# Hybrid decoder step: TensorE keeps the source's order through the units of the RWKV layer

## The chip, the core and the metric

The kernel runs on one core of a Trainium2 chip. The metric is the device time of one execution in microseconds (us). Five engines run beside each other, each with its own queue of instructions that it takes in order: TensorE (PE; its weight loads are PEld), VectorE (DVE), ScalarE (ACT), GpSimd (POOL) and SyncE (SP, which issues most DMAs). Between engines, semaphores order the work.

## What is computed

One inference step of two layers for a prompt of 1024 tokens and a group of 8 single-token samples. Layer 0 is a convolution branch and a sparse-attention branch. Layer 1, which the change touches, is RWKV-7 time mixing:

```
x_prev = concat([shift_prev, x[:, :-1]]);  xsh = x + (x_prev - x) * mu      # six mixtures
r, k, v, z = xsh[:4] @ w_rkvz                                              # four dense projections
decay = exp(-exp(-softplus(-(w0 + tanh(xsh[4] @ w1) @ w2)) - 0.5))         # low-rank (lora)
a = sigmoid(a0 + (xsh[5] @ a1) @ a2)                                       # low-rank (lora)
kk = normalised(k * k_k);  k = k * (1 + (a - 1) * k_a)
for each token t:
    sa = S @ kk[t]
    S  = S * decay[t] - sa (kk[t] * a[t])^T + v[t] k[t]^T                  # state per head, 64 x 64
    y[t] = S @ r[t]
y = group_norm(y) + sum(r * k * r_k) * v
out = (y * silu(z)) @ w_out                                                # dense, then LayerNorm
```

All values are float32. A dense product is made of three products of halves: each operand is split into a high part and a low remainder (`xh`, `xl`, `wh`, `wl`), and `xh*wh + xl*wh + xh*wl` is added up.

## The kernel before, in words

`phase_d` computes layer 1. The 1024 tokens and 16 heads are cut into 16 **units**: 8 groups of 128 tokens times 2 halves of the heads. In a unit the recurrence is worked in chunks of 64 tokens with small matrices. The work of a unit stands in four generators, which yield between their steps:

- `s1`, the **preparation** (L1329 and on): loads k, a, sigma, r of the unit (`kt`, `at`, `st_`, `rt`), builds the normalised key and the running decays (`ss` and `cum`, two sums on TensorE into the PSUM tile `sm`; pool `pm` has one buffer of it), then `KBK` and `AM` on VectorE (L1369 to L1377), then gram products into `pa` (L1396), whose evictions give `AB`, `AM`, `MRB`, then transposes into `pa` (L1419, L1420). `AB` goes out to DRAM as `md` and comes back as `MT`.
- `s2`, the **solve**: a triangular inverse of small blocks, on VectorE alone (L1433 to L1436); the result goes to DRAM (`ud`) and comes back as `UT`.
- `joinUT`, the **join**: four groups of tiny products into `pg` (L1477, L1485, L1500, L1508), with copies and 32x32 transposes on VectorE between them.
- `s3`, the **state steps**: per chunk, products with the state into `pA` and `pB`, a copy `E` on VectorE (L1529), products with `UT`, copies into `SV` (L1538, L1539), products for the new state and the output (L1547, L1548); then a group norm with two sums (L1551, L1559).

Beside the units there is a queue `F1` of **dense** generators. `t_proj(h, nm, i)` is a projection of one half of the tokens: `xmake` mixes eight tiles of input (L1207 ACT, L1208 DVE, L1211 ACT, L1212 POOL) into the pool `dx` (nine buffers each of `xh` and `xl`), `wsplit` loads and splits a weight tile of 512 KB, and 24 products (`mm3`, L1184 to L1186) make one group, sixteen groups a projection. `t_sigma` and `t_a` are the lora branches: `lora_hidden` with its own `xmake`, then small products group by group (L1276, L1294). `t_out` is the output projection of 256 tokens (groups of 12 products of 512 columns, L1772 to L1774) with LayerNorm; `t_last` that of the last 256 (L1701 to L1703). `sample_d` does the samples' step.

The loop over units runs eight **slots** per unit. A slot calls one step of `s3` of unit u, of `joinUT` and `s2` of unit u+1, of `s1` of unit u+2, and lets `run` take dense steps from `F1` for a cost of `RATE` (1.2 in the first six units, then 1.1); a step costs what it yields, 1.0 if nothing.

What sets the order on the engines: the program is traced in the order of the source, and a scheduler then arranges each engine's queue by priority and by its own estimate of when operands are ready. It may move products of different generators past each other. `tc.keep_in_program_order` pins an instruction behind the one that was traced before it on the same engine.

Of the kernel before, what the change touches and what calls it, by code (L numbers as in the profile page):

```python
# [730 lines left out]
RATE = 1.2, 1.1  # L731
# [366 lines left out]
def phase_d(nc, tc, I, O, G):  # L1098
    C = G.C
    ident = C["ident"]  # L1100
    scr = G.scr
    HV = ((slice(0, 64), 0), (slice(64, 128), 1))
    flat = lambda t: t.rearrange("p a b -> p (a b)")
    with ExitStack() as es:
# [76 lines left out]
        def mm3(dst, wh, wl, x, lo, hi):  # L1181
            xh, xl = x
            for k in range(8):
                nc.tensor.matmul(dst, lhsT=wh[:, k], rhs=xh[k][:, lo:hi], start=k == 0, stop=False)  # L1184
                nc.tensor.matmul(dst, lhsT=wh[:, k], rhs=xl[k][:, lo:hi], start=False, stop=False)  # L1185
                nc.tensor.matmul(dst, lhsT=wl[:, k], rhs=xh[k][:, lo:hi], start=False, stop=k == 7)  # L1186
# [31 lines left out]
        def lora_hidden(h, src, i):  # L1218
# [10 lines left out]
            for _, g, lo, hi in chunks(h):  # L1229
                sl, r = slice(lo, hi), hi - lo  # L1230
                ph = acc()
                for k in range(8):
                    if k < 7:
                        nc.tensor.matmul(ph[:, 0:r], lhsT=W[:, k], rhs=xh[k][:, sl], start=k == 0, stop=False)
                    nc.tensor.matmul(ph[0:64, 0:r], lhsT=W[:, k, 0:64], rhs=xl[k][:, sl], start=False, stop=False)
                    if k == 7:
                        nc.tensor.matmul(ph[:, 0:r], lhsT=W[:, k], rhs=xh[k][:, sl], start=False, stop=True)
# [12 lines left out]
        def lora_w2(nm):  # L1250
# [15 lines left out]
        def t_sigma(h):  # L1266
# [4 lines left out]
            for ti, (o, r) in enumerate(toks):  # L1271
                for c in range(2):
# [3 lines left out]
                    nc.tensor.matmul(p[0:r], lhsT=H1[:, o:o + r], rhs=A[:, sl], start=True, stop=False)  # L1276
                    nc.tensor.matmul(p[0:r], lhsT=H2[:, o:o + r], rhs=B[:, sl], start=False, stop=True)
# [6 lines left out]
        def t_a(h):  # L1284
# [3 lines left out]
            for j in range(8):  # L1288
# [3 lines left out]
                for _, g, lo, hi in chunks(h):  # L1292
                    p = acc()
                    nc.tensor.matmul(p[:, 0:hi - lo], lhsT=A[:, sl], rhs=H1[:, lo:hi], start=True, stop=False)  # L1294
                    nc.tensor.matmul(p[:, 0:hi - lo], lhsT=B[:, sl], rhs=H2[:, lo:hi], start=False, stop=True)
# [32 lines left out]
        def s1(g, d, J):  # L1328
# [21 lines left out]
            nc.tensor.matmul(ss, lhsT=K["bones"], rhs=flat(inv), start=True, stop=True)  # L1350
# [4 lines left out]
            for m in range(4):  # L1355
                nc.tensor.matmul(cum[:, m * 128:m * 128 + 128], lhsT=st_[:, m], rhs=K["tri"], start=True, stop=True)
# [21 lines left out]
            yield  # L1378
            rk = t2("inv")
            nc.vector.tensor_tensor(rk, rt, kp, op=MUL)  # L1380
# [597 lines left out]
```

## Time and profile before

| | |
|---|---|
| median of 3 runs | 2209.96 us (2204.72 to 2212.83) |
| the profiled execution | 2201.91 us, span 2200.2 us |
| granted TensorE clock, mean | 0.871 |
| busy share of PE, DVE, ACT, POOL | 84%, 68%, 52%, 44% |

The spans of the table of stretches are counted from the first instruction. The loop over units takes the second half of the span. A matmul's busy time is modelled: it includes the time from its issue until its result is through, so products that follow each other overlap, and the distance between their starts says more than their duration. The clock is granted at two levels, 1.2 and 2.4 GHz; the column PEclk is the mean share of the upper one.

### The profile page before, as it was taken

To read this page: it belongs to the slowest core of one execution; us is meant where nothing else is said; L and a number is where in the kernel's file an instruction comes from. 1 tells how busy PE (TensorE), PEld (TensorE's weight loads), DVE (VectorE), ACT (ScalarE), POOL (GpSimd) and SP (SyncE) were. 2 spreads that over 40 slices of the span, in tenths; PEclk is the share of its full clock that TensorE was granted. 3 is DMA by queue.
4 is the path that set the end of the run, shared out by engine and by line. 5 is a ranking of instruction groups with operands and counts; after the bars stand their busy time and mean duration, and the time that the engine had idled before them with its cause. 6 is when DMAs were issued, how large, how long until landed. Compare 5 with 4: busy or idle time off the path is not lost. (4 is left out here: it accounts for less than half of the span.)

```text
span 2200.2 us, 41365 instructions
## 1 busy us (share of the span) xinstructions
PE 1844.0 (84%) x16026; PEld 1545.8 (70%) x16026; DVE 1491.9 (68%) x2543; ACT 1153.6 (52%) x2359; POOL 972.8 (44%) x784
## 2 busy tenths in 40 slices
PE   5988897668999997897887999897999787987865
PEld 5987896656767886674777987695888666875543
DVE  5998995557788878226364378827748987387453
ACT  3323324544665545357466467747754575465344
POOL 4667667554655545445345212323334434113233
PEclk9998998867999876898898999897899986988956
DMA  6424344521221213546556344433544544353333
GB/s 240 132 72 142 131 151 154 200 74 33 65 59 50 58 34 97 175 126 210 167 179 204 126 118 116 145 100 117 149 130 121 180 115 135 97 155 115 119 112 103
DMA packets 232095, 275.27 MB, mean 125 GB/s; under 512 B 71545, under 2 KB 171569, under 8 KB 227738
## 3 DMA queue, kind: packets, MB, share of 16 engines
q1 hardware_dynamic: 210712, 215.21, 32.1%
q0 software_dynamic: 7616, 41.52, 5.6%
q10 hardware_dynamic: 13570, 15.90, 2.0%
q8 instruction: 126, 2.06, 0.4%
q14 instruction: 71, 0.58, 0.1%
HBM read 212.47 MB, written 64.27 MB: 126 GB/s over the span
## 5 line engine op out<-in xcount | busy, mean ns | idle before, releaser
L121 POOL TENSOR_TENSOR wl<-w,wh 128x1024 fp32r<-128x1024 f32 x81 | 200.2, 2473 | 333.5 <-ACT wh L113 317.8
L1184 PE MATMUL mm<-xh,wh 128*128 128x256 f32 (+1 forms) x1024 | 308.3, 302 | 22.6 <-ACT og L1319 9.3
L1185 PE MATMUL mm<-xl,wh 128*128 128x256 f32 (+1 forms) x1024 | 300.9, 294 | 2.0 <-POOL xl L1212 1.1
L1186 PE MATMUL mm<-xh,wl 128*128 128x256 f32 (+1 forms) x1024 | 298.5, 293 | 3.5 <-POOL wl L121 3.5
L113 ACT ACTIVATE wh<-w 128x1024 fp32r<-128x1024 f32 (+2 forms) x130 | 134.4, 1036 | 208.2 <-PE mm L1185 60.9
L1184 PEld LDWEIGHTS mm<-xh,wh 128*128 128x128 f32 x1024 | 201.9, 198 | 35.8 <-ACT og L1319 12.0
L1185 PEld LDWEIGHTS mm<-xl,wh 128*128 128x128 f32 x1024 | 203.2, 198 | 5.4 <-issue 2.0
L1186 PEld LDWEIGHTS mm<-xh,wl 128*128 128x128 f32 x1024 | 202.1, 198 | 6.3 <-POOL wl L121 4.4
L268 DVE SCALAR_TENSOR_TENSOR c<-U,cw,c 128x1024 f32<-128x1024 f32 x120 | 198.0, 1674 | 0.9
L604 POOL TENSOR_TENSOR Pl<-PT,Ph 128x512 fp32r<-128x512 f32 (+1 forms) x102 | 131.9, 1298 | 150.4 <-DVE Ph L603 123.9
L252 POOL TENSOR_TENSOR cbuf<-cbuf 128x256 f32<-128x256 f32 (+2 forms) x72 | 131.3, 1829 | 85.2 <-ACT cbuf L250 82.3
L217 PE MATMUL S<-xh,wh 128*128 128x344 f32 (+1 forms) x432 | 146.6, 339 | 21.1 <-ACT wh L113 19.4
L219 PE MATMUL S<-xh,wl 128*128 128x344 f32 (+1 forms) x432 | 145.4, 337 | 15.7 <-POOL wl L121 11.6
L218 PE MATMUL S<-xl,wh 128*128 128x344 f32 (+1 forms) x432 | 146.3, 339 | 3.8 <-POOL xl L121 3.6
L1212 POOL TENSOR_TENSOR xl<-xs,xh 128x520 fp32r<-128x520 f32 (+1 forms) x76 | 104.6, 1382 | 91.2 <-ACT xh L1211 89.1
L250 ACT ACTIVATE cbuf<-cbuf,wrow 128x256 f32<-128x256 f32 x192 | 79.3, 496 | 112.1 <-DMA cbuf<-in_ccmp,cix 70.3
L1208 DVE SCALAR_TENSOR_TENSOR xs<-xk,mu,xs 128x512 f32<-128x512 f32 x96 | 92.7, 973 | 56.4 <-ACT xs L1207 55.7
L217 PEld LDWEIGHTS S<-xh,wh 128*128 128x128 f32 (+1 forms) x432 | 85.6, 198 | 23.2 <-ACT wh L113 21.9
L562 DVE TENSOR_REDUCE nm<-S 128x1 f32<-128x640 f32 (+7 forms) x128 | 88.3, 699 | 18.9 <-PE S L558 17.7
L219 PEld LDWEIGHTS S<-xh,wl 128*128 128x128 f32 (+1 forms) x432 | 84.9, 197 | 20.1 <-POOL wl L121 13.6
L121 DVE TENSOR_TENSOR wl<-w,wh 128x1024 fp32r<-128x1024 f32 x45 | 60.4, 1341 | 54.1 <-ACT wh L113 53.9
L218 PEld LDWEIGHTS S<-xl,wh 128*128 128x128 f32 (+1 forms) x432 | 84.8, 196 | 7.1 <-POOL xl L121 4.4
(610 smaller groups left out, 5399.3 us busy)
## 6 DMA issues: line engine op xcount, KB each, us to landing
w<-in_w_rkvz SPq DMA_DIRECT2D x64, 512.0 KB
w<-in_w_out SPq DMA_DIRECT2D x36, 512.0 KB
w<-in_w_fm SPq DMA_DIRECT2D x25, 512.0 KB
xk<-x1T SPq DMA_DIRECT2D x48, 260.0 KB
xk<-x1T SPq DMA_DIRECT2D x48, 256.0 KB
w<-in_w_out SPq DMA_DIRECT2D x16, 256.0 KB
x<-in_xp SPq DMA_DIRECT2D x8, 512.0 KB
x<-x ACTq DMA_DIRECT2D x8, 512.0 KB
```

The lines of the kernel that those rows point to most:

```text
L113: nc.scalar.activation(hi, src, AF.Copy, **({} if scale is None else {"scale": scale}))
L121: e_lo.tensor_tensor(lo, src, hi, op=SUB)
L217: nc.tensor.matmul(dst, lhsT=wh[:, k, 0:n], rhs=xh[:, k, sl], start=k == 0, stop=False)
L218: nc.tensor.matmul(dst, lhsT=wh[:, k, 0:n], rhs=xl[:, k, sl], start=False, stop=False)
L219: nc.tensor.matmul(dst, lhsT=wl[:, k, 0:n], rhs=xh[:, k, sl], start=False, stop=k == 7)
L252: nc.gpsimd.tensor_tensor(bv[:, 0:n], bv[:, 0:n], bv[:, n:2 * n], op=ADD)
L268: e.scalar_tensor_tensor(c[:, i, 0:T], u[:, k:k + T], cwh[:, i, k:k + 1], c[:, i, 0:T], op0=MUL, op1=ADD)
L604: lambda: nc.gpsimd.tensor_tensor(Pl[:, 0:w], PT[:, 0:w], Ph[:, 0:w], op=SUB)]
L1184: nc.tensor.matmul(dst, lhsT=wh[:, k], rhs=xh[k][:, lo:hi], start=k == 0, stop=False)
L1185: nc.tensor.matmul(dst, lhsT=wh[:, k], rhs=xl[k][:, lo:hi], start=False, stop=False)
L1186: nc.tensor.matmul(dst, lhsT=wl[:, k], rhs=xh[k][:, lo:hi], start=False, stop=k == 7)
L1212: (nc.vector if early[0] and k % LD == 0 else nc.gpsimd).tensor_tensor(lo[k][:, 0:n], t[:, 0:n], hi[k][:, 0:n], op=SUB)
```

## The change: what it does

Inside the loop over units every product and transpose of `phase_d` on TensorE is pinned to the order of the source (`tmm`, `ttr`, switched on by `order[0] = True` just ahead of the loop). The source is put in another order to go with it: `among` runs a lora branch inside the projection that follows it; the weights of the lora branches move from the buffers `wh`, `wl` to `big`; `joinUT` starts one slot earlier but gives its first slot to VectorE alone; `s1` has one yield moved and one dropped; `t_proj` charges 2.0 for the mixing of its input, `t_out` 0.25 per pair of tiles; `RATE` is 1.3 and 0.95; `t_out(2)` enters the queue at unit 14 instead of 13.

```diff
-RATE = 1.2, 1.1
+RATE = 1.3, 0.95
...
+    order = [False]
+
+    def ordered(f):
+        def g(*a, **k):
+            x = f(*a, **k)
+            return tc.keep_in_program_order(x) if order[0] else x
+        return g
+
+    tmm, ttr = ordered(nc.tensor.matmul), ordered(nc.tensor.transpose)
...
-                nc.tensor.matmul(dst, lhsT=wh[:, k], rhs=xh[k][:, lo:hi], start=k == 0, stop=False)
+                tmm(dst, lhsT=wh[:, k], rhs=xh[k][:, lo:hi], start=k == 0, stop=False)
...
-            A = flat(wp.tile([128, 8, 128], F32R, name="wh"))
+            A = flat(bp.tile([128, 8, 128], F32R, name="big"))
...
-            B = flat(wp.tile([128, 8, 128], F32R, name="wl"))
+            B = flat(bp.tile([128, 8, 128], F32R, name="big"))
...
             W = wsplit(I["w_rkvz"][i, 0])
-            yield
+            yield 2.0
...
             nc.vector.tensor_tensor(AM[:, :, 2], v4(rt), Pv[:, :, :, 1:65], op=MUL)
-            yield
             rk = t2("inv")
             nc.vector.tensor_tensor(rk, rt, kp, op=MUL)
+            yield
...
             for m in (0, 2):
-                yield
+                if m:
+                    yield
...
                 nc.vector.transpose(U[:, o], UT[:, :, 32 * o:32 * o + 32])
+            yield
             pg = pq.tile([128, 8, 32], F32, name="pg")
...
                 if j % 2:
-                    yield
+                    yield .25
...
+        def among(proj, lora):
+            yield next(lora) or 1.5
+            yield next(proj)
+            next(lora)
+            for _ in proj:
+                next(lora, None)
+                yield 1.15
+            for x in lora:
+                yield x
...
-        F1 = [t_proj(1, "k", 1), t_sigma(1), t_proj(1, "r", 0), t_a(1), t_proj(1, "v", 2)]
+        F1 = [t_proj(1, "k", 1), among(t_proj(1, "r", 0), t_sigma(1)), among(t_proj(1, "v", 2), t_a(1))]
...
+        order[0] = True
...
-            if u == 13:
+            if u == 14:
                 F1.append(t_out(2))
...
-                if k >= 4:
+                if k >= 3:
                     step(gj[u + 1])
```

Since the products are now traced through a helper, all of them inside `phase_d` carry its line, L1106, in the changed kernel; the tiles tell them apart.

TensorE's queue around the two sums of a unit's preparation. `sm<-inv` is `ss`, `sm<-cc` is `cum`, `mm` are dense or lora products, `pB` state products, `pa` grams. Before:

```order
L1277 MATMUL mm<-wl,xl 128x512
L1276 MATMUL mm<-wh,xh 128x512
L1277 MATMUL mm<-wl,xl 128x512
L1350 MATMUL sm<-inv,cc 128x512
L1396 MATMUL pa<-AM,KBK 128x128 x4
L1521 MATMUL pB<-SV,BK 64x64 x7
L1521 MATMUL pB<-MRB,SV 64x64 x5
```

And after, in slot 2 of a unit:

```order
L1106 MATMUL mm<-xh,wl 128x264
L1106 MATMUL mm<-big,xh 128x512
L1106 MATMUL mm<-big,xl 128x512
L1106 MATMUL pB<-SV,BK 64x64 x8
L1106 MATMUL pB<-MRB,SV 64x64 x8
L1106 MATMUL sm<-inv,cc 128x512
L1106 MATMUL sm<-cc,st__13386 128x128 x4
L1106 MATMUL mm<-xh,wh 128x256
```

The state products of the slot now stand together, a pair of lora products stands behind its dense group, and `ss` and `cum` follow each other directly, where grams and pieces of state steps stood behind `ss`.

TensorE's queue where the projection of k ends and the first lora branch begins, after (the 264-column products are the projection's last, those with 64 rows are the lora branch's):

```order
L1106 MATMUL mm<-xl,wh 128x264
L1106 MATMUL mm<-xh,wl 128x264
L1106 MATMUL mm<-xh,wh 128x256
L1106 MATMUL mm<-xl,wh 64x256
L1106 MATMUL mm<-xh,wh 128x256
```

Before, joins and state steps stood between the two:

```order
L1186 MATMUL mm<-xh,wl 128x264
L1477 MATMUL pg<-U,AB 32x16 x8
L1559 MATMUL pB<-sq,cc 128x512
L1477 MATMUL pg<-U,AB 32x16 x5
L1521 MATMUL pA<-SV,AM 64x64 x8
L1477 MATMUL pg<-U,AB 32x16 x17
L1521 MATMUL pB<-AM,SV 64x64 x8
```

There are two dense groups with products of two inputs back to back now, and the unit's steps follow behind them.

VectorE's queue in slots 2 to 3, after (`kk` to `KBK` is the preparation's chain; lines of the changed kernel):

```order
L1558 TENSOR_TENSOR SV<-pB,PC 64x4x64 x2
L1362 SCALAR_TENSOR_TENSOR kk<-inv,kk 128x512
L1378 SCALAR_TENSOR_TENSOR at<-at,kk 128x512
L1382 TENSOR_TENSOR AM<-kk,P 64x4x128 x2
L1386 TENSOR_TENSOR AM<-rt,P 128x4x128
L1383 SCALAR_TENSOR_TENSOR KBK<-at,iP 128x8x64
L1384 TENSOR_TENSOR KBK<-kt,iP 64x8x64
L1385 TENSOR_TENSOR KBK<-kt,iP 64x8x64
L1540 COPY E<-pA 128x256
```

Before, at one such place:

```order
L1529 COPY E<-pA 128x256
L1353 SCALAR_TENSOR_TENSOR kk<-inv,kk 128x512
L1369 SCALAR_TENSOR_TENSOR at<-at,kk 128x512
L1539 COPY SV<-pA 64x4x64
L1436 COPY XI<-MT 64x4
L1433 TENSOR_TENSOR XT<-XI,MT 64x16
```

The copy E, which stood ahead of the chain there, now stands behind the whole of it.

## Rows read from the trace of the kernel before

**Rows 1.** Stretches: width, busy us (count) per engine, PEclk, DMA share, GB/s.

```profile
core 0: us, PE busy (x) PEld busy (x) DVE busy (x) ACT busy (x) POOL busy (x), PEclk, DMA share, GB/s
1250.00:1618.00 368.00, 333.09 (x4180) 279.98 (x4179) 245.50 (x476) 243.74 (x526) 101.87 (x120) 0.89 0.43 124
1618.00:2066.00 448.00, 383.75 (x4650) 307.52 (x4650) 323.62 (x606) 250.07 (x499) 156.71 (x127) 0.88 0.43 131
2066.00:2200.00 134.00, 82.06 (x754) 54.94 (x753) 65.16 (x131) 56.63 (x102) 42.23 (x19) 0.70 0.34 107
```

**Rows 2.** Line L1560 (once a unit): ns min/median/max, first and last start us.

```profile
L1560 ACT ACTIVATE sq<-pB,eps_gn x16: 687/687/690, 1346.0 to 2158.0; 128x512 f32<-128x512 f32 x16
```

**Rows 3.** Stretches, three short ones.

```profile
1440.00:1480.00 40.00, 40.00 (x529) 36.79 (x528) 7.56 (x15) 12.03 (x30) 8.43 (x6) 1.00 0.31 101
...
1800.00:1850.00 50.00, 33.32 (x489) 26.11 (x489) 45.77 (x80) 31.27 (x63) 26.57 (x19) 0.67 0.36 104
1850.00:1900.00 50.00, 49.91 (x579) 44.60 (x577) 18.20 (x40) 18.42 (x35) 11.57 (x9) 0.92 0.42 139
```

**Rows 4.** Stretches, one of dense products alone.

```profile
1240.00:1245.00 5.00, 5.00 (x45) 5.00 (x44) 0.25 (x1) 1.71 (x3) 2.29 (x1) 1.00 0.14 52
```

**Rows 5.** Waits of TensorE, 1250 to 2200: us in total, times, longest.

```profile
PE pa L1396 <- DVE KBK L1375: 11.8, 4, 3.2
...
PE sm L1356 <- ACT inv L1351: 4.1, 3, 2.8
```

**Rows 6.** Chain that ended last: start us, us, what.

```profile
1711.50 0.65 PE pg L1477 x38
...
1716.19 1.08 PE pB L1521 x32
...
1721.75 0.86 PE pA L1551 x2
1723.23 1.09 PE pa L1396 x16
...
2060.16 1.09 PE sm L1384 x8
...
2078.82 1.92 DMA ud<-XI
...
2084.77 1.71 DMA UT<-ud
```

**Rows 7.** Timeline of ScalarE: start us, us, engine, line, operation.

```profile
1764.05 1.28 ACT L1351 ACT_TABLE_LOAD   x1
1765.35 0.69 ACT L1351 ACTIVATE inv<-sm,eps_kk 128x512 f32<-128x512 f32 x1
1766.05 1.28 ACT L1352 ACT_TABLE_LOAD   x1
1767.35 0.63 ACT L1352 ACTIVATE inv<-inv 128x512 f32<-128x512 f32 x1
```

**Rows 8.** Groups by line, VectorE, 1250 to 2066: busy us, mean ns.

```profile
L1208 DVE SCALAR_TENSOR_TENSOR xs<-xk,mu,xs 128x512 f32<-128x512 f32 x45 | 42.4, 944 | 8.9 <-ACT xs L1207 8.7
L1373 DVE TENSOR_TENSOR AM<-kk,P 64x512 f32<-64x512 f32 x30 | 32.5, 1083 | 0.7 <-PE pB L1521 0.4
...
L1369 DVE SCALAR_TENSOR_TENSOR at<-at,kk 128x512 f32<-128x512 f32 x15 | 16.7, 1113 | 0.2
...
L1374 DVE SCALAR_TENSOR_TENSOR KBK<-at,iP 128x512 f32<-128x512 f32 x15 | 12.3, 820 | 0.6 <-ACT iP L1362 0.6
...
L1529 DVE COPY E<-pA 128x256 f32<-128x256 f32 x28 | 11.7, 420 | 8.7 <-PE pA L1521 8.3
...
L1353 DVE SCALAR_TENSOR_TENSOR kk<-inv,kk 128x512 f32<-128x512 f32 x15 | 10.4, 691 | 15.1 <-ACT inv L1352 14.9
L1377 DVE TENSOR_TENSOR AM<-rt,P 128x512 f32<-128x512 f32 x15 | 10.3, 690 | 0.2
```

**Rows 9.** Stretches, the loop's first 50 us.

```profile
1250.00:1300.00 50.00, 48.81 (x496) 43.22 (x494) 31.48 (x67) 31.00 (x68) 7.64 (x12) 1.00 0.43 121
```

**Rows 10.** Mixing of inputs: GpSimd's group; L1211 by stretch; one stretch.

```profile
L1212 POOL TENSOR_TENSOR xl<-xs,xh 128x520 fp32r<-128x520 f32 (+1 forms) x76 | 104.6, 1382 | 91.2 <-ACT xh L1211 89.1
...
1343.00:1367.00 24.00, 4.33 (x7) 0.86 0.41 125
1387.00:1431.00 44.00, 5.61 (x9) 0.77 0.47 136
...
1387.00:1431.00 44.00, 37.99 (x458) 29.50 (x459) 38.53 (x74) 33.08 (x70) 20.49 (x23) 0.77 0.47 136
```

More of the change, by code (lines that the diff above doesn't have):

```diff
@@ L1275, in t_sigma @@
                     sl = slice(c * 512, c * 512 + 512)
-                    nc.tensor.matmul(p[0:r], lhsT=H1[:, o:o + r], rhs=A[:, sl], start=True, stop=False)
-                    nc.tensor.matmul(p[0:r], lhsT=H2[:, o:o + r], rhs=B[:, sl], start=False, stop=True)
+                    tmm(p[0:r], lhsT=H1[:, o:o + r], rhs=A[:, sl], start=True, stop=False)
+                    tmm(p[0:r], lhsT=H2[:, o:o + r], rhs=B[:, sl], start=False, stop=True)
                     dst = otile()[:, 0:512]
@@ L1349, in s1 @@
             ss = pm.tile([128, 512], F32, name="sm")
-            nc.tensor.matmul(ss, lhsT=K["bones"], rhs=flat(inv), start=True, stop=True)
+            tmm(ss, lhsT=K["bones"], rhs=flat(inv), start=True, stop=True)
             nc.scalar.activation(flat(inv), ss, AF.Ln, bias=C["eps_kk"])
@@ L1355, in s1 @@
             for m in range(4):
-                nc.tensor.matmul(cum[:, m * 128:m * 128 + 128], lhsT=st_[:, m], rhs=K["tri"], start=True, stop=True)
+                tmm(cum[:, m * 128:m * 128 + 128], lhsT=st_[:, m], rhs=K["tri"], start=True, stop=True)
             P = up.tile([128, 8, 65], F32, name="P")
@@ L1383, in s1 @@
             for m in range(4):
-                nc.tensor.matmul(rb[:, m * 128:m * 128 + 128], lhsT=BR[:, 4 * d + m], rhs=rk[:, m], start=True, stop=True)
+                tmm(rb[:, m * 128:m * 128 + 128], lhsT=BR[:, 4 * d + m], rhs=rk[:, m], start=True, stop=True)
             nc.vector.tensor_tensor(bv, rb.rearrange("p (j t) -> p j t", j=4), VF[:, :, 64:192], op=MUL)
@@ L1395, in s1 @@
                         for h, i in HV:
-                            nc.tensor.matmul(gr[i][:, mm, c], lhsT=flat(KBK[h, m + mm, c, 1 - i:3 - i]),
+                            tmm(gr[i][:, mm, c], lhsT=flat(KBK[h, m + mm, c, 1 - i:3 - i]),
                                              rhs=AM[h, m + mm, i::2 - i, c], start=True, stop=True)
@@ L1520, in s3 @@
             MH = [(m, h, i) for m in range(4) for h, i in HV]
-            mm = lambda out, lhsT, rhs, start: nc.tensor.matmul(out, lhsT=lhsT, rhs=rhs, start=start, stop=True,
+            mm = lambda out, lhsT, rhs, start: tmm(out, lhsT=lhsT, rhs=rhs, start=start, stop=True,
                                                                 skip_group_check=True)
@@ L1550, in s3 @@
             yc = (py_ if YC else pm).tile([128, 512], F32, name="pA" if YC else "sm")
-            nc.tensor.matmul(yc, lhsT=K["cent"], rhs=flat(Y), start=True, stop=True)
+            tmm(yc, lhsT=K["cent"], rhs=flat(Y), start=True, stop=True)
             ycv = yc.rearrange("p (m t) -> p m t", m=4)
@@ L1558, in s3 @@
             var = (py_ if YC else pm).tile([128, 512], F32, name="pB" if YC else "sm")
-            nc.tensor.matmul(var, lhsT=K["bones"], rhs=flat(sq), start=True, stop=True)
+            tmm(var, lhsT=K["bones"], rhs=flat(sq), start=True, stop=True)
             nc.scalar.activation(flat(sq), var, AF.Ln, scale=1.0 / 64, bias=C["eps_gn"])
@@ L1579, in sample_d @@
             ss = pm.tile([128, 512], F32, name="sm")
-            nc.tensor.matmul(ss[:, 0:64], lhsT=K["bones"], rhs=flat(inv), start=True, stop=True)
+            tmm(ss[:, 0:64], lhsT=K["bones"], rhs=flat(inv), start=True, stop=True)
             nc.scalar.activation(flat(inv), ss[:, 0:64], AF.Ln, bias=C["eps_kk"])
@@ L1591, in sample_d @@
             rb = pm.tile([128, 512], F32, name="sm")
-            nc.tensor.matmul(rb[:, 0:64], lhsT=K["bones"], rhs=flat(inv), start=True, stop=True)
+            tmm(rb[:, 0:64], lhsT=K["bones"], rhs=flat(inv), start=True, stop=True)
             tt(bvs, w3(rb[:, 0:64]), v, op=MUL)
@@ L1636, in sample_d @@
             var = pa_.tile([128, 512], F32, name="pa")
-            nc.tensor.matmul(var[:, 0:64], lhsT=K["bones"], rhs=sq, start=True, stop=True)
+            tmm(var[:, 0:64], lhsT=K["bones"], rhs=sq, start=True, stop=True)
             nc.scalar.activation(sq, var[:, 0:64], AF.Ln, scale=1.0 / 64, bias=C["eps_gn"])
@@ L1700, in part @@
                         yh, yl = (x[kk][:, 128 * ti:128 * ti + 128] for x in y)
[L1701 to L1703 removed]
+                        tmm(p[ti][f], lhsT=yh, rhs=a, start=kk == 0, stop=False)
+                        tmm(p[ti][f], lhsT=yh, rhs=b, start=False, stop=False)
+                        tmm(p[ti][f], lhsT=yl, rhs=a, start=False, stop=kk == 7)
             def join(ti):
```

41 lines of the change are left out of this document (19 added, 22 removed).

## The prediction

> **What bounds the kernel now.** I read the table of stretches first, cut at the ends of units 5 and 13 of the loop that the change touches, then the waits of TensorE, then short windows. The loop and what follows take 950 of the 2200.2 us: 368 to the end of unit 5, 448 for units 6 to 13, 134 for the rest [rows 1]. The first mark of a unit's end lies at 1346.0 and the last at 2158.0, so 15 units take 812 us, 54 each [rows 2]. No engine is full. In units 6 to 13 TensorE shows 383.75 us busy of 448, VectorE 323.62 and ScalarE 250.07; in units 0 to 5 it is 333.09, 245.50 and 243.74 of 368 [rows 1]. VectorE's work is thus 41 us a unit in both stretches.
>
> The busy time of TensorE is not its work. A dense product of 256 columns comes every 5.00/45 = 0.111 us in a run without gaps at full clock [rows 4]; while the clock stands at half, the same work shows twice as much. Busy time by granted clock gives the work at full clock: 333.09 x 0.89 = 296 us in the first stretch, 383.75 x 0.88 = 338 in the second. So the first stretch is 296 of work, 35 idle and 37 lost at half clock; the second 338, 64 and 46.
>
> What wastes the loop is that two kinds of work take turns where they could overlap. From 1440 to 1480 TensorE is busy all of 40 us and VectorE 7.56; from 1800 to 1850 VectorE is busy 45.77 of 50 and TensorE 33.32, at a clock of 0.67; from 1850 to 1900 TensorE 49.91 and VectorE 18.20 [rows 3]. The order in which TensorE takes its instructions sets this: dense groups run in a row of their own, and then come stretches where everything that TensorE has left waits for VectorE's chains. The waits agree: the largest in total is for KBK, which VectorE makes last in a unit's preparation [rows 5].
>
> **The change, part by part.** *Work.* No product is added or dropped; the order shows only places. A unit's low-rank part, by rows: 168 state products at 1.08/32 = 0.034 us, 192 join products at 0.65/38 = 0.017, 32 gram products at 1.09/16 = 0.068 and 32 transposes at no more than that, three 512-column fp32 sums at 0.86 for the two passes of each, 16 passes of 128 columns at 1.09 for 8 [rows 6]. That is 5.7 + 3.3 + 2.2 + 2.2 + 2.6 + 2.2 = 18 us. A dense group of 24 is 24 x 0.111 = 2.7 us. So units 6 to 13 are 8 x 18 + 32 groups x 2.7 + 16 groups of 12 at 512 columns (an estimate: twice 0.111 each, 2.7 a group) = 144 + 86 + 43 = 273 us, against 338 by busy time and clock. The difference is what modelled ends of lone products add. I take the middle, 306, and in the same way for the first stretch (6 x 18 + 48 x 2.7 + about 22 of lora products + 18 of the first units' preparation = 278, against 296) 287.
>
> *The gain: steps in slots.* Per slot TensorE now has one state step, then join and preparation steps, then 2.7 us of dense work. The state step's answer needs one VectorE copy (0.42) or two, so a group covers it. What it doesn't cover, in units 6 to 13: (a) the two sums of a preparation (`ss`, then `cum`) now stand directly behind each other, and both use the single buffer `sm`. `cum` waits until ScalarE has read `ss`: a table load of 1.28 and the Ln of 0.69 [rows 7], 2.0 us in each of 14 units, 28 us in all. Before, such waits came three times in the loop, 4.1 us together [rows 5], because other products were put between. Queued behind `cum` on TensorE are the slot's dense group and the next state step. (b) In VectorE's order the copy E of slot 3 stands behind the preparation's chain: 0.69 + 1.11 + 2 x 1.08 + 0.69 + 0.82 + two of at most 0.82 [rows 8], 7.1 us, which can start only when ScalarE has done Ln, a table load and Exp (1.28 + 0.69 + 1.28 + 0.63 = 3.9 us [rows 7]). That is 11.0 + 0.4 us from `ss` on. TensorE reaches the product that needs E after 0.4 (`ss`) + 2.0 + 1.1 (`cum`) + 2.7 + 0.6 (18 products) + 2.7 = 9.5 us. So 2 us are open, and more when VectorE is late. (c) The triangular solve of the next unit on VectorE waits for two DMA hops through DRAM, each 1.7 to 1.9 us [rows 6], and stands ahead of a state copy: 1 to 5 us, taken as 3. Together 7 us a unit, 56 in the stretch. Half clock cost 37 us beside 35 idle, and 46 beside 64; I take 0.6 of the idle time, 34, since these waits are short and spread. 306 + 56 + 34 = 396 instead of 448: **52 us gained**. The ends: VectorE's own 324 below, and 448 or slightly more above, if each slot waits for VectorE as it does now.
>
> *The start.* The preparation of units 0 and 1, the solve and the join of unit 0 are not held in order, but the dense groups of the loop now stand behind them. Before, TensorE was busy 48.81 of 50 us there, at full clock [rows 9], since it could take dense groups early. The chain is gram, eviction, two DMA hops, solve, two hops, four join steps: about 35 us, of which 18 are TensorE's own work. I put 17 us of new idle time there (0 if other parts of the first projection still cover it, 25 at most).
>
> *Five hand-overs.* When one projection ends and the next input is mixed, eight tiles pass ScalarE, VectorE (0.94 [rows 8]) and GpSimd (1.38 [rows 10]) into buffers that the old projection has just left. At GpSimd's rate this is 8 x 1.38 = 11 us. In source order only the low-rank steps between the two groups hide it: 2 to 6 us. I take 5 us of waiting each, 25 in all; the ends are 0, and what the tiles took before, 24 us for seven and 44 for eight with the first of the next input [rows 10], when nothing hurried them because other products went by. The fifth lies at the start of unit 6 and is counted here. Six times (a) is 12, and I add 4 for the rest. So the first stretch is 287 + 17 + 12 + 25 + 4 = 345, and 0.6 of the 58 idle us among it (35) for half clock: 380 instead of 368: **12 us lost**. The low-rank products (lora) cost nothing of their own: they ride behind dense groups, and their weights have left the buffers of the dense weights, so no dense weight waits for them.
>
> *The last units.* Dense groups run out in unit 13, then 108 products stand in one lump in the first slot of unit 14, and 60 in that of unit 15, ahead of the state chain. Before, they were strewn in. The lump delays the chain, the clock before was only 0.70 there [rows 1], and the same weights must come. I take 0, with 20 us either way.
>
> **Sum.** The profiled execution took 2201.91 us (span 2200.2). 2201.9 + 12 - 52 = 2162. Its time lies 8 us under the median of 2209.96, so in the terms of the median: 2170.
>
> The clock deserves a look of its own. Where TensorE was busy 33.32 of 50 us the clock was 0.67, and 0.92 where it was 49.91 [rows 3]. The Trainium skill, "TensorE: Matmul & The Clock Gate", section "HAM oscillation — how this bites in real kernels", says that a loop whose bursts of products are shorter than the waits between them falls back to half clock in every round. That speaks against waits in every slot; the trace agrees in the windows named. Its result is the last rival.
>
> **The rivals.** *VectorE becomes the bound.* If TensorE never holds it up, units 6 to 13 take VectorE's 324 us instead of my 396: 2170 - 72 = 2098. For it speaks that VectorE is near 92% busy from 1800 to 1850; against it that half of its chains start from TensorE.
>
> *The hand-overs block everything (slower).* TensorE now stands at the first dense product of a new input, and state steps, joins and preparations of the unit queue behind it, which earlier went past. If the tiles take what they took before, a mean of (24 + 44)/2 = 34 us less 4 of cover, five cost 150 instead of 25: 2170 + 125 = 2295. The point from which it decides is 25 + 40 = 65 us, 13 each; from 15 each on the loss can be measured. For it: ScalarE and VectorE were busy 33.08 and 38.53 of 44 us in such a stretch [rows 10]; against it: much of that was units' work that now stands still too, so the tiles get the engines.
>
> *Gains and losses cancel*: 2199 to 2221, if the hand-overs cost 11 to 15 us each, or if the second stretch gives 4 to 6 us a unit less than I took.
>
> *Half clock through spread waits.* At 0.67 in units 6 to 13 [rows 3] the 306 us of work take 457, plus 56: 513 instead of 396, 2287.
>
> **How the numbers follow.** My forecast, 2105 to 2199, has 0.49; VectorE as the bound 0.14; no change 0.13; the hand-overs, from 15 us each on, 0.19; half clock 0.05. A measurement of this kernel can tell about 0.5% (11 us) from no change: faster 0.49 + 0.14 = 0.63, same 0.13, slower 0.24. The range goes down to VectorE's bound, 2098, and up to 2245, where hand-overs cost 20 us each; about one in ten is left out on either side.
>
> **What would show it.** In the changed kernel's table of stretches: the distance of the ends of units in the second half (I say 49 us, before 56); a wait of `sm` for ScalarE's `inv` in each of 14 units, about 28 us in all; idle time of TensorE between the last projection of the first half and the first state step, about 17 us; and five waits of dense products for `xh` or `xl` of 5 us each. I am wrong if units 6 to 13 still take 54 us or more, or if the waits for `xh` and `xl` pass 65 us. If the gain is there and the first stretch is also shorter, the hand-overs were priced too high.

## The result: 2313 us, slower by 4.6%

The changed kernel took 2313.39 us (median of 4 runs, 2309.56 to 2323.61), the kernel before, on the same chip, 2211.39 (4 runs, 2204.72 to 2222.01): a ratio of 1.046, with a 95% interval of 1.041 to 1.052. The prediction said 2170, with a range up to 2245. The sign was wrong.

The profiled execution of the changed kernel took 2317.03 us (span 2315.3). Up to the loop the two kernels do the same work in the same time (by 1250 us TensorE has done 6468 products in the one trace and 6462 in the other); the loop and what follows it take 1065 us now, 950 before. The table of stretches of the changed kernel, cut at the ends of units 5 and 13 like [rows 1] (width, busy us and count per engine, granted clock, DMA share, GB/s):

```profile
core 0: us, PE busy (x) PEld busy (x) DVE busy (x) ACT busy (x) POOL busy (x), PEclk, DMA share, GB/s
1250.00:1686.00 436.00, 337.64 (x4268) 284.45 (x4267) 228.69 (x447) 239.88 (x516) 103.25 (x118) 0.82 0.36 107
1686.00:2160.00 474.00, 358.22 (x4525) 290.72 (x4527) 319.20 (x621) 250.57 (x498) 140.81 (x123) 0.82 0.39 118
2160.00:2315.00 155.00, 96.50 (x784) 63.29 (x780) 63.14 (x138) 60.55 (x102) 48.65 (x22) 0.76 0.32 105
```

TensorE's busy time in the three stretches is 337.64 + 358.22 + 96.50 = 792 us, and was 333.09 + 383.75 + 82.06 = 799. Its idle time is 1065 - 792 = 273 us, and was 950 - 799 = 151. So by these sums the loss, 115 us in the profiled executions, is time in which TensorE has nothing that it may start: 63 us more in units 0 to 5, 52 more in units 6 to 13, and 7 more in the rest. Busy time did not grow, at nearly the same number of products (9577 and 9584), although the granted clock fell (0.82 for 0.89 and 0.88) and a lower clock stretches it. By the prediction's measure, busy time times clock, the two things that make it up moved against each other: in the first two stretches half clock takes 61 + 64 = 125 us, before 37 + 46 = 83, and what the measure calls work is 277 + 294 = 571 us, before 296 + 338 = 634. Why the second fell is not shown.

What it waits for, in the two stretches. TensorE's waits of the changed kernel, 1250 to 1686 (us in total, times, longest), the first rows:

```profile
PE mm L1106 <- ACT xh L1220: 22.7, 14, 4.0
PE mm L1106 <- POOL xl L1221: 22.6, 25, 2.4
PE sm L1106 <- ACT inv L1360: 13.0, 6, 2.4
```

And from 1686 to 2160:

```profile
PE sm L1106 <- ACT inv L1360: 27.2, 8, 6.3
PE pA L1106 <- DVE E L1540: 23.3, 9, 5.9
PE sm L1106 <- DVE sinv L1601: 11.2, 1, 11.2
PE pa L1106 <- DVE MRB L1412: 10.2, 8, 3.1
PE mm L1106 <- DVE xl L119: 7.0, 4, 3.0
```

In [rows 5] no wait of the whole loop passed 11.8 us in total. In the first stretch it is now the freshly mixed input, `xh` and `xl`. In the second it is the units' own chain: `inv` (the wait of `cum` for ScalarE's Ln of `ss`), E, MRB; and one wait of 11.2 us for the step of the samples (`sinv`), which is pinned into the row like everything else. The waits listed for this stretch add up to 115.7 us, its whole idle time (474 - 358 = 116): the pin costs nothing here beside waits for operands.

One unit shows what a fixed order does. This is the timeline of the changed kernel in slots 2 and 3 of one unit (start us, us, engine, line, operation; in brackets the idle time before it and who ended it):

```profile
1895.44 2.36 POOL L121 TENSOR_TENSOR wl<-w,wh 128x1024 fp32r<-128x1024 f32 x1
...
1896.47 1.88 DVE L1217 SCALAR_TENSOR_TENSOR xs<-xk,mu,xs 128x512 f32<-128x512 f32 x1 [0.72 <-DMA xk<-x1T]
...
1896.88 1.12 PE L1106 MATMUL sm<-inv,cc 128*128 128x512 f32 x2
...
1899.62 0.64 ACT L1220 ACTIVATE xh<-xs 128x520 fp32r<-128x520 f32 x1 [3.19 <-DVE xs L1219]
...
1901.53 1.28 ACT L1360 ACT_TABLE_LOAD   x1
...
1902.82 0.69 ACT L1360 ACTIVATE inv<-sm,eps_kk 128x512 f32<-128x512 f32 x1
...
1903.56 2.07 PE L1106 MATMUL sm<-cc,st__18535 128*128 128x128 f32 x8 [5.56 <-ACT inv L1360]
...
1905.29 0.77 PE L1106 MATMUL mm<-wh,xh 128*128 128x512 f32 x1
...
1910.81 0.60 PE L1106 MATMUL pB<-SV,ident 64*64 64x256 f32 x4
...
1914.34 1.25 DVE L1383 SCALAR_TENSOR_TENSOR KBK<-at,iP 128x512 f32<-128x512 f32 x1
...
1916.12 0.41 DVE L1540 COPY E<-pA 128x256 f32<-128x256 f32 x1
...
1916.59 1.12 PE L1106 MATMUL pA<-E,UT 64*64 64x64 f32 x16 [5.17 <-DVE E L1540]
```

`ss` is through at 1898.0. ScalarE cannot read it yet: it stands 3.19 us at a tile of the next input's mixing, for VectorE, and comes to the table load at 1901.53 and to Ln at 1902.82. `cum` starts at 1903.56, 5.56 us after TensorE fell idle. Behind `cum` stood a dense group that needed nothing of all this (the last split of a weight tile, `wl` at 1895.44, is done at 1897.8); it runs from 1905 on and ends before 1910. Then E, which needs only one copy, waits behind VectorE's preparation chain, whose last part (KBK, 1914.34) is done at 1915.6, and behind pieces of LayerNorm and of the samples' step among it: 5.17 us more. The dense group in between covered nothing of the first wait and a part of the second, since it was fixed in that place.

### The profile page after: what moved, and what is told of

The parts are those of the page before. It is cut to its first block, busy times and chain, and to the rows that moved or that the text cites. A ratio compares the mean times of both kernels' runs of the same rounds, so it can differ in the third digit from the quotient of the medians.

```text
span 2315.3 us, 41365 instructions
## 1 busy us (share of the span) xinstructions
PE 1828.1 (79%) x16026; PEld 1530.7 (66%) x16026; DVE 1477.0 (64%) x2543; ACT 1160.9 (50%) x2359; POOL 968.3 (42%) x784
## 5 line engine op out<-in xcount | busy, mean ns | idle before, releaser
L1106 PE MATMUL mm<-xh,wh 128*128 128x256 f32 (+1 forms) x1088 | 339.8, 314 | 42.0 <-ACT xh L1220 23.6
L1106 PE MATMUL mm<-xl,wh 128*128 128x256 f32 (+3 forms) x1088 | 329.0, 304 | 28.9 <-POOL xl L1221 27.2
L1106 PE MATMUL mm<-xh,wl 128*128 128x256 f32 (+1 forms) x1024 | 301.9, 295 | 2.9 <-POOL wl L121 2.9
L1106 PEld LDWEIGHTS mm<-xh,wh 128*128 128x128 f32 x1088 | 225.3, 208 | 64.8 <-ACT xh L1220 29.1
L1106 PEld LDWEIGHTS mm<-xl,wh 128*128 128x128 f32 (+1 forms) x1088 | 220.3, 203 | 38.1 <-POOL xl L1221 35.8
L1106 PEld LDWEIGHTS mm<-xh,wl 128*128 128x128 f32 x1024 | 208.1, 203 | 3.1 <-POOL wl L121 3.1
L602 ACT ACTIVATE PT<-mm 128x512 f32<-128x512 f32 (+1 forms) x102 | 59.5, 586 | 61.6 <-PE mm L590 45.5
```

The costliest lines, as they stand in the source:

```text
L1106: x = f(*a, **k)
```

## The experiments

The theory (A in the expectations) was that the fixed order itself costs the time: TensorE stands at one product while others that are ready stand behind it. The rivals: the rewriting of the source around it (`among`, `RATE`, the moved steps) costs it; or it is one wait alone (the hand-overs of inputs, `cum`, E, the lump of products at the end). Each expectation says what its letters stand for. The runs were made on several chips, and the kernel before took 2200 to 2211 us on them (medians), so a difference of some 10 us between runs on two chips tells little; where it matters, the ratio to the kernel before on the same chip is given.

**Everything but the pin.** One line is taken out of the changed kernel:

```diff
-        order[0] = True
```

> The changed kernel with all its edits but the pin: the scheduler arranges TensorE's queue freely in the units again. Theory A (the pin costs the time: at a hand-over TensorE stands at the first product of a new input and the units' steps queue behind it, and ss/cum stand back to back): the loss of 102 us goes, 2190 to 2240 us, and the wait of sm for inv falls from 40.2 us to under 10. Rival B (the rewritten source order, the RATE and the moved joins cost it, whoever sets the queue): stays at 2280 to 2320 us.

Measured: 2191.61 us, against 2209.75 of before on the same chip, a ratio of 0.991 [0.989, 0.994]. So the pin costs 2313.4 - 2191.6 = 122 us, and the other edits together are a gain of 18, a small one (0.9%), but clear of the noise. The wait for `inv` all but goes (0.8 us in all). The stretches of the profiled execution, which at 2208.89 us was the slowest of ten (2179.46 to 2208.89):

```profile
1250.00:1600.00 350.00, 315.42 (x4004) 256.72 (x4003) 236.69 (x466) 226.70 (x487) 95.61 (x114) 0.89 0.40 117
1600.00:2055.00 455.00, 394.92 (x4829) 324.38 (x4828) 341.12 (x625) 266.10 (x542) 154.81 (x129) 0.88 0.44 135
2055.00:2207.00 152.00, 99.76 (x757) 63.59 (x757) 62.54 (x122) 59.66 (x100) 52.21 (x23) 0.76 0.35 113
```

Idle time is 957 - 810 = 147 us in this execution, about what it was before the change (151), and 126 less than with the pin. The rival that blamed the source is out. What this leaves open: the scheduler also arranges the queues of the other engines, around a pinned row or a free one, and no run separates TensorE's order from theirs.

**Which products' order costs?** Two kernels pin half of the products among themselves and leave the scheduler to merge the two halves: in the first the products of `s1`, `joinUT` and `s3`, in the second the dense and lora products.

```diff
-            return tc.keep_in_program_order(x) if order[0] else x
+            if order[0]:
+                if last[0] is not None:
+                    tc.add_manual_dep(x.ins, last[0], mybir.DependencyInfo(
+                        mybir.DependencyClass.NoSync, mybir.DependencyReason.DATA), reason="own order")
+                last[0] = x.ins.name
+            return x
```

> Only the units' products (preparation, join, state) keep the source's order among themselves; dense, lora and sample products are free. Theory A: dense products no longer hold up units and the other way round, so most of the loss goes: 2200 to 2250 us. Rival C (the units' own order is too tight: cum behind ss, state steps behind VectorE's chain): 2270 us or more.

> Only the dense, lora and output products keep the source's order among themselves; the units' products are free. Theory A: units pass a waiting dense product, 2190 to 2240 us. Rival: if the order among dense and lora products itself costs (mixing of an input is not hidden because no other dense work may go by), 2270 us or more.

Measured, one execution each on the chip of the kernel without a pin: 2261.27 and 2230.88 us, 70 and 39 over it, where its own ten runs spread over 29. The units' order among themselves is already the larger part; the two make 109 of the 122. The first lies between the bands that had been set for it, the second within A's. With only the units pinned, TensorE may go past a unit's wait with dense products, but not with another step of the units, and the waits (1250 to 2260) are those of the chain:

```profile
PE pA L1108 <- DVE E L1550: 27.1, 11, 8.4
PE pa L1108 <- DVE MRB L1422: 26.8, 12, 13.1
```

**Where along the loop?** The pin is switched on only at unit 6, or off again at unit 13; the first edit is shown.

```diff
-        order[0] = True
         for u, (g, d) in enumerate(units):
+            order[0] = u >= 6
```

> The changed kernel with the pin only from unit 6 on. Theory A: the first stretch (units 0 to 5, five of the hand-overs) gets back its 65 to 70 us and the rest keeps the loss of the second half: 2235 to 2260 us, the end of unit 5 near 1618 instead of 1686. Rival D (the loss is spread evenly, by the waits inside each unit): the first stretch gets back 40 us or less, 2270 us or more.

> The changed kernel with the pin off from unit 13 on. Theory A2 (the lumps of 108 and 60 products ahead of the state chain, kept in place by the pin, cost the last units): 2275 to 2295 us, and the distance from the end of unit 13 to the last instruction falls from 155 to 120 to 135 us. Rival (the last units wait for weights and inputs in any order): 2300 us or more.

Measured, one execution each: 2251.21 us pinned from unit 6 on, 60 over the version without a pin and 62 under the changed kernel: each half of the loop carries about half of the cost. Unpinned from unit 13 on: 2311.26, no different from 2313.4, and from the end of unit 13 to the last instruction it is 159 us, 155 in the changed kernel, where theory A2 had 120 to 135. No gain for the last units shows.

**The hand-overs.** In these two kernels the mixing of the inputs of sigma, r, a and v in units 0 to 5 is left out: these products take the tiles mixed for k (and the two lora branches share one pair of tiles for their hidden values). They compute something else and serve as a probe only. The first has the pin, the second has not.

```diff
+            if h == 1 and i != 3 and 'x' in kept:
+                return kept['x']
```

> The changed kernel without the mixing of four inputs in units 0 to 5 (the lora branches and the projections of r and v take the mixed input of k; that work is left out). Theory A (hand-overs): with no input to wait for the time falls by 70 us or more, to 2200 to 2245 us, nearly all of it before the end of unit 5. Rival D (waits inside the units): it falls by 30 us or less, 2280 us or more.

> The same work left out of the kernel of e1 (all edits, no pin; 2191.61 us). Theory A: there the units go past the mixing, so it is worth 35 us or less, 2155 to 2190 us. Rival D: it is worth as much as in the pinned kernel, within 20 us.

Measured, one execution each on one chip: 2254.70 with the pin (59 less than with the mixing) and 2170.36 without (21 less). The kernel before took 2200.51 there, in its one run, 9 to 11 less than beside the two kernels with the mixing; by the ratios the two differences are 48 and 11. Four hand-overs are therefore worth 12 to 15 us each under the pin, 3 to 5 each without it, and the difference, 59 - 21 = 38 us (48 - 11 = 37), is what the pin adds at them. The 59 lies under the 70 that A had put there, and the 38 over the 20 up to which the two would have counted as equal. Under the pin the fall lies before the end of unit 5, as A had said: 371.5 us there for 436, and in the other stretches 476.5 for 474 and 155 for 155. The two kernels have the same work in the same stretches, so their tables give the rest of the pin's cost like for like. With the pin:

```profile
1250.00:1621.50 371.50, 314.94 (x4277) 275.31 (x4276) 191.24 (x390) 201.12 (x456) 54.11 (x58) 0.89 0.35 105
1621.50:2098.00 476.50, 358.11 (x4527) 291.01 (x4527) 319.15 (x621) 249.55 (x496) 141.78 (x123) 0.82 0.39 117
2098.00:2253.00 155.00, 97.26 (x778) 64.28 (x776) 63.13 (x138) 60.88 (x103) 48.69 (x22) 0.75 0.32 104
```

Without:

```profile
1250.00:1584.00 334.00, 308.50 (x4206) 264.37 (x4205) 194.65 (x392) 201.94 (x455) 56.01 (x58) 0.94 0.39 115
1584.00:2014.00 430.00, 358.95 (x4549) 289.60 (x4548) 334.88 (x639) 248.66 (x501) 139.68 (x122) 0.85 0.43 130
2014.00:2169.00 155.00, 101.00 (x758) 66.36 (x757) 61.25 (x120) 59.46 (x99) 52.75 (x23) 0.74 0.33 106
```

371.5 - 334 = 37.5 us in units 0 to 5, 476.5 - 430 = 46.5 in units 6 to 13, nothing in the rest: 84, and 38 at the hand-overs, is the 122. TensorE's busy time in units 6 to 13 is equal (358.11 and 358.95), with nearly as many products; all 46.5 us are idle time. The waits there (1621.5 to 2098, with the pin):

```profile
PE sm L1106 <- ACT inv L1372: 27.8, 8, 5.5
PE pA L1106 <- DVE E L1552: 26.4, 9, 5.9
```

Without it (1584 to 2014) the wait for `inv` is not among the nine largest, and that for E is:

```profile
PE pA L1106 <- DVE E L1552: 9.3, 6, 3.0
```

**Is it one wait?** If so, it should go with its cause. First `cum` is moved one step ahead of `ss`, so that nothing stands behind its wait for Ln.

```diff
-            yield
-            ss = pm.tile([128, 512], F32, name="sm")
...
             cum = pm.tile([128, 512], F32, name="sm")
...
+            yield
+            ss = pm.tile([128, 512], F32, name="sm")
```

> The changed kernel with cum (and what reads it) moved one slot ahead, so that ss no longer stands directly ahead of it at the single buffer sm. Theory A1 (the wait of sm for inv, 40.2 us in 14 units, lies on the path): 2265 to 2290 us and that wait under 10 us. Rival (the wait only stands in for VectorE's chain, which then makes the state step wait as long): 2300 us or more, and the waits for E and KBK grow by about as much.

Then E goes from VectorE to ScalarE, past the chain it stood behind:

```diff
-                nc.vector.tensor_copy(E, pA[:, 0])
+                nc.scalar.activation(E, pA[:, 0], AF.Copy)
```

> The changed kernel with one edit: the copy E of the state steps is made by ScalarE instead of VectorE, so that it no longer stands behind the preparation's chain in VectorE's queue (step (b) of the prediction). In the changed kernel TensorE waits 25.3 us for E in 11 cases, 23.3 us of them in units 6 to 13. Theory A2 (the order in which VectorE reaches E is a cause of its own): most of the 23 us go, with the half clock behind them, and the time falls by 20 to 40 us from 2313, to 2270 to 2295. Rival (VectorE's whole chain is what TensorE stands behind, and E is only the first product that shows it): the wait for E shrinks but those for SV, MRB, KBK or inv grow by nearly as much, and the time stays above 2300. Slower than 2320 if E now stands behind ScalarE's table loads.

And both:

> The changed kernel with the two edits that were made one at a time before: cum one step ahead of ss, and the copy E on ScalarE. Alone they gave 13 and 2 us. If each took away a wait of its own and the other one filled in, the two together give more than the sum: 2260 to 2285, with the idle time of TensorE in units 6 to 13 under 95 us (114 to 116 in the others). If it is the whole round trip between TensorE, VectorE and ScalarE that the fixed order exposes, and each removal only moves the wait to the next product (theory A3), the sum is no more than their sum: 2290 to 2305, idle time 105 to 120 us, and the waits for MRB, SV, U or Y grow by what those for inv and E lose.

Measured: 2300.58, 2311.53 and 2287.83 us (ratios to before of 1.048 [1.044, 1.053] for the second and 1.037 [1.033, 1.040] for the third; the first is one execution, 1.045 times the one of before on its chip). Against the changed kernel's 1.046 the first two are no measurable gain, 13 and 2 us by the times as they stand, though a wait of 40.2 us in all (`inv`, the whole loop) is gone from the first and one of 25.3 (E) from the second but for 1.5. TensorE's idle time in units 6 to 13 is 114 us in either, 116 in the changed kernel. Both times lie in the rivals' bands. Where the waiting went, first `cum` ahead of `ss` (E was 25.3, MRB 11.2 in the changed kernel):

```profile
PE pA L1106 <- DVE E L1540: 37.7, 15, 7.6
...
PE pa L1106 <- DVE MRB L1412: 26.0, 7, 10.8
```

and with E on ScalarE (SV was 10.4):

```profile
PE pa L1106 <- DVE MRB L1412: 21.0, 13, 5.0
PE pB L1106 <- DVE SV L1550: 16.3, 7, 4.6
```

Both edits together are a gain of 26 us as the times stand, 22 by the ratios (1.037 for 1.046, each known to about half a per cent, so 7 to 37), of 65.5 us of waits, of which 13.7 stayed as a wait for ScalarE's E. In the kernel with both, the stretch of units 6 to 13:

```profile
1676.00:2127.00 451.00, 343.04 (x4537) 278.68 (x4539) 324.51 (x607) 254.38 (x514) 146.00 (x123) 0.84 0.40 123
```

and TensorE's waits over the whole loop (1250 to 2370):

```profile
PE pa L1106 <- DVE MRB L1412: 16.5, 12, 5.8
PE pA L1106 <- ACT Y L1559: 15.7, 6, 6.2
PE pB L1106 <- DVE SV L1550: 15.3, 9, 4.4
PE pA L1106 <- ACT E L1540: 13.7, 8, 4.6
...
PE pA L1106 <- DVE SV L1558: 10.6, 6, 2.9
```

Idle time in units 6 to 13 is 451 - 343 = 108 us, 8 less than in the changed kernel, where the waits for `inv` and E made 50.5 of 116; the other 15 us that the stretch lost are busy time, at a clock of 0.84 for 0.82. The wait for `inv` is no longer among the largest; MRB (11.2 us in the changed kernel), Y (11.0) and SV of L1550 (10.4) have each grown by 5, and SV of L1558 (0.5) by 10. The time as it stands fell between the two bands, 2 us under what "only moves" allowed (2290); scaled by the kernel before to the changed kernel's chip it is 2292 to 2295, inside that band. Most of the removed waiting came back at the next product in the row.

**Is the dense group too short?** In units 6 and on two groups per slot instead of one:

```diff
-RATE = 1.3, 0.95
+RATE = 1.3, 1.9
```

> The changed kernel with RATE 1.3, 1.9 instead of 1.3, 0.95: in units 6 and on a slot takes two dense groups (5.4 us) instead of one (2.7), so the queue of dense groups lasts for units 6 to 9 and leaves units 10 to 13 bare. A slot then has 18/8 + 5.4 = 7.7 us of TensorE's work, a unit 61. If a group that is too short to cover the round trips is the cause of the second half's loss (A3), units 6 to 9 come near that, 62 to 68 each with an idle share under 12%, and units 10 to 13 take what VectorE needs, 41 to 52: the time is 2285 to 2320 in all. If waits stay as long beside larger groups (a wait that has nothing to do with cover, such as DMA hops or buffers), units 6 to 9 take 72 or more with an idle share of 20% or more as before, and the time passes 2335.

Measured: 2363.77 us, a ratio of 1.072 [1.067, 1.078]. Units 6 to 9 take 348 us, 87 each, and the four bare units after them 173, 43 each:

```profile
1685.00:2033.00 348.00, 247.75 (x2693) 205.54 (x2689) 223.07 (x400) 160.89 (x308) 120.37 (x94) 0.82 0.40 123
2033.00:2206.00 173.00, 113.45 (x1817) 83.61 (x1818) 103.71 (x222) 89.61 (x191) 20.72 (x31) 0.70 0.27 77
```

The bare units are as A3 said, the full ones are not: 29% of them is idle. The waits in 1685 to 2033 tell why:

```profile
PE mm L1106 <- ACT wh L113: 27.2, 1, 27.2
PE sm L1106 <- ACT inv L1360: 12.3, 4, 6.4
PE mm L1106 <- DVE og L1325: 10.9, 5, 3.6
```

E is not among the eleven largest, so the longer group does cover that wait. In the bare units (2033 to 2206) it is the largest:

```profile
PE pA L1106 <- DVE E L1540: 27.0, 8, 7.2
```

The wait for `inv` is about as long as before in the full units, 3 us each. In its place the dense products wait for their own operands: the weights `wh` once for 27 us, free places in `og`, input tiles. In a fixed order these waits, too, hold up the units. So A3's "too short" holds for E alone, and the rival's waits, which have nothing to do with cover, are the larger part; the time, the 87 us a unit and the idle share all lie on the rival's side, and without the one wait of 27 us a unit would still take 80.

**The end of the loop.** The version without the pin, with `t_out(2)` entering at unit 13 as before the change.

> The version without the pin (all other edits kept), and t_out(2) enters the queue at unit 13 as in the kernel before. It came to 2191.6 with unit 14. If the entry at 14 starves TensorE of dense groups at the end (the last units took 152 us there against 134 before), the last stretch falls by 10 to 20 us: 2172 to 2182. If the scheduler, which is free to move products, fills the last units either way, or the dense groups run out at the same time, nothing changes: 2185 to 2198.

Measured: 2193.72 us, a ratio of 0.995 [0.992, 0.998], against 0.991 with unit 14. Nothing is gained. All kernels with the new source take 152 to 162 us after unit 13 where the kernel before took 134 [rows 1]; only this last one takes 145, and its units 6 to 13 take 463 us, 8 more than with unit 14. By the counts, more dense products in `mm` are left for the end (144 in the changed kernel, 82 before, in the rows of that tile); that this is the cause was not tested by itself.

## Why the prediction was wrong

By its own sum, in the terms of the two stretches:

| | idle, said | idle, measured | busy, said | busy, measured |
|---|---|---|---|---|
| units 0 to 5 | 58 | 98 | 322 | 338 |
| units 6 to 13 | 56 | 116 | 340 | 358 |
| the rest | as before, 52 | 58.5 | as before, 82 | 96.5 |

(Busy, said, is work and half clock together: 380 - 58 and 396 - 56.) The three stretches took 155 us more than said, and 106 of them, two thirds, are idle time.

The step that failed is the idle term of the sum. For units 6 to 13 it put (a) to (c) at 56 us and all other waits, 64 us of idle time before, at nothing. Measured in the changed kernel, `inv`, E and U make 27.2 + 23.3 + 2.2 = 53 us together, near the 56, but by luck: the first two were put too low and (c) far too high. The other 63 us of the 116 are the waits put at nothing. In units 0 to 5 two terms failed: the hand-overs (45 us of waits, where the four of them had 20), and the 4 us for the rest, which are about 25 once the start, `inv`, `xh` and `xl` are taken from the 98. The terms one by one:

- **The start**: 17 us of idle time said. From 1250 to 1300 TensorE is now busy 33.30 of 50 us, 16.7 idle, where it was busy 48.81 [rows 9]. Right, and the clock was 0.59 there. Without the pin the same 50 us show 47.79 us busy, so the order is what costs it.

```profile
1250.00:1300.00 50.00, 33.30 (x429) 28.51 (x429) 27.10 (x65) 18.16 (x45) 1.86 (x4) 0.59 0.19 43
1375.00:1430.00 55.00, 28.17 (x193) 18.37 (x192) 36.20 (x65) 35.37 (x63) 26.75 (x30) 0.60 0.40 116
1535.00:1580.00 45.00, 22.19 (x154) 15.20 (x154) 28.90 (x57) 28.82 (x49) 19.81 (x26) 0.59 0.43 127
1690.00:1730.00 40.00, 19.94 (x133) 15.14 (x135) 24.43 (x47) 20.39 (x37) 7.08 (x9) 0.63 0.34 99
```

- **Step (a), `cum` behind `ss`**: 2.0 us in each of 14 units, 28 in all, said; 40.2 us in 14 waits measured, 13.0 in the six units of the first stretch (said 12) and 27.2 in the eight of the second (said 16). The place and the count were right. The size failed where ScalarE was not at the Ln at once: the step took the table load and Ln by themselves, and ScalarE has a row of its own, with mixing and evictions ahead of them (seen in the one unit shown above).
- **Step (b), E behind the chain**: 2 us a unit, 16 in the second stretch, said; 23.3 measured, up to 5.9 in one. The same failure: the sum of 11.4 us against 9.5 had VectorE start the chain on time and do nothing else between, and VectorE did mixing, LayerNorm and the samples' step.
- **Step (c)**, 3 us a unit for solve and DMA hops, 24 in the stretch: the wait for `U` is 2.2 us there, that for SV of L1550 4.5; what came instead is MRB (10.2) and one wait of 11.2 us for `sinv`. The samples' step was named nowhere in the prediction, though it is pinned like the rest.
- **The premise behind (a) to (c) is the step that failed most**: that what a fixed order wastes is the sum of the few waits that a group does not cover, and that the old waits, 64 us of idle time there, vanish. The experiments with `cum` and E say otherwise: taking away 52 of 65.5 us of named waits gave 22 to 26. In such a row every round trip between TensorE and the two other engines is a place to wait, and a wait that is removed shows the next one. Without the pin, TensorE had filled them with whatever was ready: for the same work, 71 us of idle time instead of 118 (430 - 359, 476.5 - 358).
- **The five hand-overs**: 5 us each, 25, said; the waits for `xh` and `xl` of the mixing make 25.2 + 23.6 = 48.8 over the loop, 45.3 of them in units 0 to 5, 11 for each of the four there (the fifth, at unit 6, has 3.5: TensorE stood there for `sinv` more than for the input), and the kernels without the mixing price the four at 12 to 15 each under the pin. The mark of 65 us at which the rival would decide was not passed by the waits; by time, the four cost 48 to 59. So the mechanism of that rival (TensorE at the first product of a new input, the unit's steps behind it) was at work at or a little under its "from 15 each on" and far from its 34, and alone it would have made about a quarter of the miss: 38 us more than without the pin.
- **Work and half clock**: I said 287 and 306 us of work, and 0.6 of the idle time, 35 and 34 us, for half clock. By the same measure the changed kernel has 277 and 294 of work, both lower, and 61 and 64 us at half clock, which is 0.62 and 0.56 of its 98 and 116 us of idle time. So the 0.6 held, and half clock cost more only because the idle time did. The rival's 0.67 throughout units 6 to 13 was not seen: 0.82; a time near its 2287 came about by idle time for the most part. In the four windows above (the start and three hand-overs) the clock was 0.59 to 0.63, where TensorE is busy half to two thirds of the time. The Trainium skill ("TensorE: Matmul & The Clock Gate", section "HAM oscillation — how this bites in real kernels") tells of a kernel whose bursts of products are shorter than the waits between them and which falls back to half clock in every round. The four windows agree with it as far as they go; whether each burst in them is shorter than its wait was not measured.
- **VectorE as the bound** was far off: 319 us busy of 474.
- **The last units**: 0 said, within 20; 21 us lost, but about as much in the other kernels with the new source (18 without the pin), so not by the lumps of the fixed order.
- "I am wrong if units 6 to 13 still take 54 us or more": they take 474/8 = 59. This was the right mark; the other, 65 us of waits for `xh` and `xl`, was not reached.

What the prediction read rightly was that work of two kinds took turns [rows 3]. It concluded that an order by hand would overlap them better. The kernel without the pin shows that the new source, its order as a hint only, gains 18 us, and that making the order binding loses 122. How much of the 18 comes from the order and how much from `RATE`, the buffers of the lora weights or the other edits was not tested.

What stays open: how much of the 46.5 us in units 6 to 13 belongs to each wait, since they stand in for each other; whether more buffers for `xh` and `xl` would take the hand-overs away under the pin, which was not tried; what part the queues of VectorE and ScalarE have, which the scheduler also arranges; and the last 18 to 21 us of the end.

## What to carry to other kernels

A fixed order on an engine's queue turns every late operand into a stop for all that stands behind it; price it by the longest round trips through the other engines' own queues, with everything that those have ahead, and not by the durations of the operations that are waited for. Hand a scheduler a better source order first, and pin only what it gets wrong: here the same source was 18 us faster than before with the order as a hint, and the order as a rule cost 122. When a named wait is removed and the time does not follow, look at which wait has grown in its place before removing the next.

## What the hardware showed that was not expected

`cum`, eight passes of 128 columns, shows the clock directly. The passes of the changed kernel in two units, the first after a wait of 2.8 us, the second after one of 4.1 (ns: min/median/max, then first and last start):

```profile
L1106 PE MATMUL sm<-cc,st__19215 x8: 275/275/377, 1965.1 to 1965.9; 128*128 128x128 f32 x8
L1106 PE MATMUL sm<-cc,st__19868 x8: 421/421/581, 2021.1 to 2022.7; 128*128 128x128 f32 x8
```

The column PEclk is the mean clock as a share of 2.4 GHz, so half clock throughout shows as 0.50; from 1903.5 to 1905.3, where `cum` runs in the unit of the timeline above, it is 0.50. Five of the eight units from 1686 on have the 421: the four whose wait for `inv` was 4.1 to 6.3 us and one that waited 1.4; the three with 275 waited 1.4 to 2.8. The price of a stop can also come later: in the first of the two units `cum` runs at full clock, but from 1966.4 to 1969.7 the clock is 0.51, and the dense products behind `cum` start 0.22 us apart instead of 0.12.

And a unit that has no dense work beside it still takes 43 us in a fixed order, with 34% of it idle and the clock at 0.70 (2033 to 2206 in the kernel with two groups per slot). TensorE is busy 113 of these 173 us and VectorE 104: neither engine fills the time, the steps that wait for each other do.
